# Input projections on raw, unnormalised tokens, with 1/rms put in where results leave PSUM, in a two-layer hybrid trunk on one core

## The chip, the core and the metric

The kernel runs on one core of a Trainium2 chip. A core has five engines with queues of their own: TensorE (PE in the rows; its weight loads are PEld), VectorE (DVE), ScalarE (ACT), GpSimd (POOL) and SyncE (SP), which here only issues DMAs. The metric is the device time of one execution in microseconds (us).

## What is computed

Two layers over one sequence of 2048 tokens, model width 1024, all in float32. Cut to what matters here:

```python
for l in range(DEPTH):                      # DEPTH = 2
    h = rmsnorm(x, norm_g[l])               # x * rsqrt(mean(x*x) + EPS) * g
    z = h @ w_in[l]                         # 1024 -> 2512 columns
    (g_q, g_k, g_v, g_lr, g_gate,           # 256, 256, 512, 16, 512
     c_q, c_kv, k_pe, m_gate) = jnp.split(z, split_idx, axis=-1)   # 256, 128, 64, 512
    log_a = log_sigmoid(g_lr @ w_gla_gate_up[l] + b_gla_gate[l]) / 16
    o_gla = gla_mix(g_q, g_k, g_v, log_a, gla_norm_g[l]) * silu(g_gate)
    # c_q and c_kv go through an RMSNorm of their own, then through w_uq and w_ukv;
    # k_pe gets the rotary turn; causal attention with 4 heads gives o_mla
    o_mla = attention(c_q, c_kv, k_pe) * silu(m_gate)
    x = x + concat([o_gla, o_mla]) @ w_out[l]
```

## The kernel before

Tokens are handled in 16 tiles of 128 (names `t`, `a`, `b`), in 8 pairs `p`; the model width is 8 slices of 128 (index `k`). A float32 product is made of three matmuls on a high and a low part (`mm3`, lines 97 to 99). `block(ps, hT, w, n, ins)` issues the 8 slices of one projection of one tile, 24 matmuls 464 or 512 columns wide, and calls after slice `k` whatever work `ins[k]` lists. So the text of the program sets where each small piece of work stands among the matmuls.

Each layer has four phases. **Pass 1** makes for each pair the blocks `mi a`, `mi b`, `qk a`, `v a`, `qk b`, `v b`. `mi` holds the latents, the rotary key and the 16 low-rank gate columns (columns 448 to 463). `lat_chain(t)` (lines 415 to 433) reads `mi` out of PSUM; its first two operations make `lr`, the gate columns. `gates_a(t)` (line 442) transposes `lr` on TensorE, `gates_b` (449) multiplies it by a small weight `w3r` into `lg`, `gates_c` (458) makes cumulative sums. `gla_b(t)` (476) takes `qk` out of PSUM into `qkp`, which TensorE transposes next. `tail(t)` ends a tile of the linear attention with a normalisation `osn`. **Pass 2** makes the blocks `gt` and `mg` (the two SiLU gates) and the attention queries; a tile's gate output `on` is transposed by TensorE in `out_t`. **Phase b** is the attention, **phase c** the output projection: it writes the new residual stream to the DRAM tensors `xd`, and sums over slices of squares to `sd`.

Before pass 1 uses a tile, the class `Prep` (lines 350 to 396) normalises it. `x` loads the transposed tile, `s` (first layer only) squares it on ScalarE and folds the eight slices into one 128x128 tile `ss` (on VectorE for tile 0, on GpSimd for the others), `n` adds up `ss` over partitions with one matmul by a 128x128 matrix of ones, so that 1/rms comes out for all tokens in every partition (`rb`, 128x128, through a chain of six operations in `rsq`), and `h` (two halves) multiplies the tile by it, splits it into high and low part (`hT`) and writes the normalised tile to the DRAM tensors `hd`, from which pass 2 reads it again. In phase c the same is done ahead for the first two tiles of layer 2.

What sets the order: in pass 1 and pass 2 TensorE follows the program; within the first pair and its loads ScalarE and VectorE do too (`manual_schedule(engines=BOOT)`). Elsewhere a scheduler orders the engines when the kernel is built. SyncE issues DMAs in one queue, in an order that the scheduler sets as well. The input weights are loaded in pieces of two slices, `mi` from two column ranges.

Of the kernel before, what the change touches and what calls it, by code (L numbers as in the profile page):

```python
# [19 lines left out]
P = 128  # L20
# [33 lines left out]
def trunk(ctx: ExitStack, tc: tile.TileContext, xT, positions, norm_g, w_in, w_up, b_up, gla_g,  # L54
# [19 lines left out]
    ones = cp.tile([P, P], F32, name="ones")  # L74
# [4 lines left out]
    sspe = cp.tile([P, NT], F32, name="sspe")  # L79
# [3 lines left out]
    xd = [dp.tile([P, KT, QD], F32, name=f"xd{q}") for q in range(NQD)]  # L83
# [40 lines left out]
    def silu(pool, z, tag, a=None):  # L124
        a = logsig(pool, z, 512, tag, a=a)
# [4 lines left out]
    hd = [dp.tile([P, KT, P], F32, name=f"hd{t}") for t in range(NT)]  # L130
# [217 lines left out]


    class Prep:  # L350
        def __init__(self, l, x_tile, small, psum):
            self.l, self.xt, self.small, self.psum = l, x_tile, small, psum
            self.xs, self.ss, self.rb, self.hT = {}, {}, {}, {}

        def x(self, t):
# [28 lines left out]

        def h(self, t, half):
            if half == 0:
                self.hT[t] = hT_tile("hT")
            hT, xt = self.hT[t], self.xs[t]
            ks = slice(half * 4, half * 4 + 4)
            xv = xt.rearrange("p (k c) -> p k c", k=KT)[:, ks, :]  # L390
            V.tensor_tensor(out=xv, in0=xv, in1=self.rb[t].unsqueeze(1).broadcast_to([P, 4, P]), op=ALU.mult)
            A.activation(out=hT[:, 0, ks, :], in_=xv, func=AF.Copy)
            V.tensor_tensor(out=hT[:, 1, ks, :], in0=xv, in1=hT[:, 0, ks, :].bitcast(F32), op=ALU.subtract)
            if half == 1:
                dma(hd[t].rearrange("p k c -> p (k c)"), xt)
                del self.xs[t], self.rb[t]


    def pass1(l, wp, pp, w1, lat, hT01):
# [8 lines left out]
        prep = Prep(l, lambda name: x_tile(wp, name), w1, lambda: pp.tile([P, P], F32, tag="tp", name="tp"))  # L408
        prep.hT.update(hT01)
        hTs = prep.hT  # L410

        def sq_tile():
            return wp.tile([P, D], F32, tag="stg", name="sq", bufs=3)

        def lat_chain(t, mi):
            lt = lr[:, t % 2]
            V.tensor_copy(lt[:, 0:3:2, 0:16], mi[:, 448:464].unsqueeze(1).broadcast_to([P, 2, 16]))
            V.tensor_tensor(out=lt[:, 1, 0:16], in0=mi[:, 448:464], in1=lt[:, 0, 0:16].bitcast(F32), op=ALU.subtract)
            v2 = w1.tile([P, 2], F32, name="v2")
            jk = w1.tile([P, 256], F32, tag="jk", name="jk", bufs=1)  # L420
            A.activation(out=jk, in_=mi[:, 0:256], func=AF.Square, scale=1.0 / 16.0, accum_out=v2[:, 0:1])
            A.activation(out=jk[:, 0:128], in_=mi[:, 256:384], func=AF.Square, scale=128.0 ** -0.5,
                         accum_out=v2[:, 1:2])
            A.activation(out=jk[:, 128:192], in_=mi[:, 384:448], func=AF.Square, scale=192.0 ** -0.5,
                         accum_out=sspe[:, t:t + 1])
# [6 lines left out]
            V.tensor_tensor(out=kpe[:, t, :], in0=mi[:, 384:448], in1=sm["gkr"], op=ALU.mult)  # L432
# [158 lines left out]
        def sqs(t):  # L591
            return [lambda: prep.s(t, sq_tile(), G)] if l == 0 else []

        def pair(p):
# [5 lines left out]
                  merge(bt[0], tail(a - 1) if p else {}, {0: [go(prep.h, b, 0)], 2: [go(prep.h, b, 1)]} if p else  # L600
                        {2: [go(prep.n, b), go(prep.h, b, 0)], 3: [go(prep.h, b, 1)]} if l == 0 else {}))
# [6 lines left out]
            block(mi, hTs[b], wi["mi"], 464, merge({3 if p else 5: [go(gates_a, a)], 5 if p else 7: [go(gates_b, a)]}, bt[1]))  # L608
# [6 lines left out]
            if not more:  # L615

                for which, blks in (("gt", (2, 3)), ("mg", (4, 5))):
                    pc = wi_pieces(l, which, pool_stage(wp, 2)(512))
# [23 lines left out]
        with tc.manual_schedule(engines=BOOT):  # L642
            if l == 0:
# [7 lines left out]
                for load, _ in pm[1:]:  # L651
                    load()
# [682 lines left out]
```

## Time and profile before

| | us |
|---|---|
| runs of the kernel | 2302.77, 2305.85, 2309.09 (median 2305.85) |
| the profiled execution | 2303.08 |
| its span | 2301.2, mean granted clock 0.995 |
| busy in the span: PE, DVE, ACT, POOL | 2238.2 (97%), 1463.3 (64%), 1328.6 (58%), 452.7 (20%) |
| pass 1 of layer 1 / pass 2 / phase b / phase c | to about 390 / 600 / 985 / 1164 |
| pass 1 of layer 2 / pass 2 / phase b / phase c | to about 1520 / 1700 / 2130 / the end |

The four rows of stages are read from which lines TensorE runs. PE is idle for 63 us in all. The granted clock is a share of TensorE's full speed: 1.00 is 2.4 GHz, 0.50 is 1.2 GHz.

### The profile page before, as it was taken

How to read it: one execution, taken by the hardware profiler on the slowest of the kernel's cores; microseconds unless marked ns; L12 is line 12 of the kernel's file. 1: busy time of each engine (PE TensorE's matmuls, PEld its weight loads, DVE VectorE, ACT ScalarE, POOL GpSimd, SP SyncE). 2: the span in 40 equal slices, each digit the busy share in tenths (PEclk: the TensorE clock that was granted, in tenths of full speed). 3: DMA queues.
4: the chain of work that ended last, by engine and by line, in shares of the span. 5: the costliest groups of instructions: out<-in, count | busy, mean ns of one | idle time of the engine just before them, and what ended most of it. 6: DMA issues, size and time to landing. Idle time of an engine off the chain costs nothing.

```text
span 2301.2 us, 37516 instructions
## 1 busy us (share of the span) xinstructions
PE 2238.2 (97%) x12629; PEld 1931.6 (84%) x12629; DVE 1463.3 (64%) x4456; ACT 1328.6 (58%) x3648; POOL 452.7 (20%) x685
## 2 busy tenths in 40 slices
PE   6999999999999999999999999999999999999999
PEld 4788887888899988888878888878888999988887
DVE  6586676665788887742356566666657888785211
ACT  5465556666777777642245555567667777676100
POOL 1110111333312122132200000033332122123100
PEclk9999999999999999999999999999999999999999
DMA  5121124443311111166432112254432111113542
GB/s 171 46 79 60 47 87 142 129 133 110 108 37 50 31 47 54 51 209 191 146 100 79 61 60 85 75 158 128 134 94 90 31 54 41 33 55 106 176 133 83
DMA packets 186310, 213.09 MB, mean 93 GB/s; under 512 B 18419, under 2 KB 131814, under 8 KB 186118
## 3 DMA queue, kind: packets, MB, share of 16 engines
q1 hardware_dynamic: 185702, 210.58, 29.0%
q8 instruction: 100, 1.64, 0.3%
q14 instruction: 92, 0.75, 0.1%
q0 software_dynamic: 416, 0.12, 0.0%
HBM read 129.91 MB, written 80.74 MB: 92 GB/s over the span
## 4 chain that ended last, share of the span: by engine, by line
PE 87%; ACT 5%; DVE 5%; DMA 1%; issue 1%; POOL 0%; SPq 0%; ACTq 0%; DVEq 0%; POOLq 0%
PE tp L94 8%; PE co L98 5%; PE co L99 5%; PE co L97 5%; PE sp L975 3%; PE sp L978 3%; PE sp L979 3%; PE sp L977 3%; PE sp L976 2%; PE gt L99 2%; PE gt L97 2%; PE gt L98 2%; PE o L1050 2%; PE mg L99 2%; PE mg L97 2%; PE mg L98 2%
## 5 line engine op out<-in xcount | busy, mean ns | idle before, releaser
L98 PE MATMUL co<-y,wo_h 128*128 128x512 f32 x512 | 199.3, 389 | 0.8 <-POOL y L1156 0.8
L97 PE MATMUL co<-y,wo_h 128*128 128x512 f32 x512 | 199.6, 390 | 0.2 <-ACT y L1155 0.2
L99 PE MATMUL co<-y,wo_l 128*128 128x512 f32 x512 | 199.3, 389 | 0.0
L986 DVE TENSOR_SCALAR_CACHE_REDUCE p<-sp 128x512 f32<-128x512 f32 (+5 forms) x304 | 172.9, 572 | 23.0 <-PE sp L979 18.5
L1203 DVE TENSOR_TENSOR xc<-co,xc 128x512 f32<-128x512 f32 x64 | 44.1, 689 | 211.5 <-PE co L99 177.4
L993 ACT ACTIVATE p<-p,nm 128x128 f32<-128x128 f32 (+15 forms) x128 | 154.0, 1204 | 36.4 <-DVE nm L992 30.0
L1029 DVE TENSOR_TENSOR pl<-tp,ph 128x512 fp32r<-128x512 f32 x224 | 151.7, 686 | 35.5 <-ACT ph L1028 34.2
L1050 PE MATMUL o<-pl,v 128*128 128x256 f32 x576 | 170.1, 295 | 2.0 <-DVE pl L1029 1.2
L1048 PE MATMUL o<-ph,v 128*128 128x256 f32 x576 | 167.9, 292 | 4.3 <-ACT ph L1028 2.9
L1028 ACT ACTIVATE ph<-tp 128x512 fp32r<-128x512 f32 x224 | 130.3, 592 | 71.1 <-PE tp L94 63.1
L94 PE MATMUL tp<-cst,p 128*128 128x128 f32 x1088 | 165.7, 274 | 0.3 <-DVE pl L1029 0.2
L1049 PE MATMUL o<-ph,v 128*128 128x256 f32 x576 | 161.1, 280 | 0.0
L975 PE MATMUL sp<-kn,q 128*128 128x512 f32 (+3 forms) x320 | 129.4, 405 | 7.6 <-ACT q L910 5.0
L94 PEld LDWEIGHTS tp<-cst,p 128*128 128x128 f32 x1088 | 124.6, 140 | 8.7 <-DVE pl L1029 1.2
L1048 PEld LDWEIGHTS o<-ph,v 128*128 128x128 f32 x576 | 108.9, 189 | 11.4 <-ACT ph L1028 4.5
L1007 POOL TENSOR_SCALAR gt<-gt,rl 128x128 f32<-128x128 f32 x128 | 78.5, 623 | 195.3 <-DVE rl L1005 108.2
L977 PE MATMUL sp<-kn,q 128*128 128x512 f32 (+3 forms) x320 | 116.4, 370 | 0.0
L976 PE MATMUL sp<-kn,q 128*128 128x512 f32 (+3 forms) x320 | 116.2, 363 | 0.0
L1050 PEld LDWEIGHTS o<-pl,v 128*128 128x128 f32 x576 | 108.6, 189 | 8.2 <-DVE pl L1029 3.6
L978 PE MATMUL sp<-kr,q 128*128 128x512 f32 (+3 forms) x320 | 115.0, 366 | 0.3
L979 PE MATMUL sp<-kr,q 128*128 128x512 f32 (+3 forms) x320 | 114.5, 368 | 0.0
L98 PEld LDWEIGHTS co<-y,wo_h 128*128 128x128 f32 x512 | 96.1, 188 | 21.0 <-POOL y L1156 1.2
(285 smaller groups left out, 6731.1 us busy)
## 6 DMA issues: line engine op xcount, KB each, us to landing
hd<-xt SPq DMA_DIRECT2D x32, 512.0 KB, 2.6
hf<-hd SPq DMA_DIRECT2D x32, 512.0 KB, 3.7
stg<-in_w_in SPq DMA_DIRECT2D x28, 512.0 KB, 4.5
yst<-yd SPq DMA_DIRECT2D x28, 512.0 KB, 5.1
qd<-qs SPq DMA_DIRECT2D x32, 384.0 KB, 3.0
gst<-qd SPq DMA_DIRECT2D x64, 192.0 KB, 2.5
xt<-in_xT SPq DMA_DIRECT2D x16, 512.0 KB, 4.3
od<-osn SPq DMA_DIRECT2D x32, 256.0 KB, 2.1
```

The lines of the kernel that those rows point to most:

```text
L94: T.transpose(o, i, ident[:k, :k])
L97: T.matmul(o, lhsT=lh, rhs=rh, start=start, stop=False)
L98: T.matmul(o, lhsT=lh, rhs=rl, start=False, stop=False)
L99: T.matmul(o, lhsT=ll, rhs=rh, start=False, stop=stop)
L975: T.matmul(o, lhsT=qn[:, 0, ts_], rhs=kn[:, 0, k0:k1], start=True, stop=False)
L976: T.matmul(o, lhsT=qn[:, 0, ts_], rhs=kn[:, 1, k0:k1], start=False, stop=False)
L977: T.matmul(o, lhsT=qn[:, 1, ts_], rhs=kn[:, 0, k0:k1], start=False, stop=False)
L978: T.matmul(o, lhsT=qrr[:, 0, ts_], rhs=kr[:, c0:c1], start=False, stop=False)
L979: T.matmul(o, lhsT=qrr[:, 1, ts_], rhs=kr[:, c0:c1], start=False, stop=True)
L986: V.tensor_scalar(out=pt[:, c0:c0 + w], in0=sp[:, 0:w], scalar1=0.0, scalar2=-3e38, op0=ALU.add, op1=ALU.max, accum_out=mx[:, m:m + 1])
L1048: T.matmul(o[:, s], lhsT=vh, rhs=ph[:, j, s], start=(kb == 0), stop=False)
L1050: T.matmul(o[:, s], lhsT=vh, rhs=pl[:, j, s], start=False, stop=(last and j == 1))
```

## The change

Five things change. (1) `hT` is made from the raw tile: a copy to the high part (ScalarE) and a subtraction (VectorE). 1/rms is kept per token, in three forms in `rt[:, t, 0:3]` (r, r/8, r squared), and applied where projections leave PSUM. (2) The sum of squares: in layer 1 GpSimd squares and folds each tile (`prep_s`), and the reducing matmul has `ss` as stationary side and a 128x2 matrix of ones as moving side, so that 1/rms comes out with one token in each partition. It stands after slice 7 of `mi a` and after slice 6 of `mi b`. In layer 2, one load (`load_s`) and one `norm_q` serve four tiles, after slice 4 of `mi a` in every second pair. (3) The `hd` tensors are gone: pass 2 loads the raw tile. (4) The weights come as five arrays laid out by group, the tokens also as an array `xt` laid out by tile, and `xd` is laid out by tile. (5) The first loads come in another order. In pass 2 the SiLU takes r: its smaller operations are split anew, and one of them goes to GpSimd.

```diff
-        def s(self, t, sq, eng):
-            A.activation(out=sq, in_=self.xs[t], func=AF.Square, scale=1.0 / 32.0)
-            for n in (512, 256):
-                eng.tensor_tensor(out=sq[:, 0:n], in0=sq[:, 0:n], in1=sq[:, n:2 * n], op=ALU.add)
...
-        def n(self, t):
-            ps = self.psum()
-            T.matmul(ps, lhsT=ones, rhs=self.ss.pop(t), start=True, stop=True)
...
-            V.tensor_tensor(out=xv, in0=xv, in1=self.rb[t].unsqueeze(1).broadcast_to([P, 4, P]), op=ALU.mult)
-            A.activation(out=hT[:, 0, ks, :], in_=xv, func=AF.Copy)
-            V.tensor_tensor(out=hT[:, 1, ks, :], in0=xv, in1=hT[:, 0, ks, :].bitcast(F32), op=ALU.subtract)
-            if half == 1:
-                dma(hd[t].rearrange("p k c -> p (k c)"), xt)
+    def split_x(xs, hT, half, lo=None):
...
+        A.activation(out=hT[:, 0, ks, :], in_=xv, func=AF.Copy)
+        (lo or V).tensor_tensor(out=hT[:, 1, ks, :], in0=xv, in1=hT[:, 0, ks, :].bitcast(F32), op=ALU.subtract)
+    def norm(pool, ps, ss, t, n):
+        for i in range(n):
+            T.matmul(ps[:, 2 * i:2 * i + 2], lhsT=ss[:, i * P:(i + 1) * P], rhs=ones, start=True, stop=True)
+        v = pool.tile([P, n], F32, tag=f"xv{n}", name="xv")
+        V.tensor_scalar(out=v, in0=ps[:, 0:2 * n:2], scalar1=1.0 / D, scalar2=EPS, op0=ALU.mult, op1=ALU.add)
+        r = pool.tile([P, n], F32, tag=f"xs{n}", name="xs")
+        rsq(pool, v, n, r, f"xr{n}")
+        V.tensor_copy(rt[:, t:t + n, 0], r)
+        V.tensor_scalar(out=rt[:, t:t + n, 1], in0=r, scalar1=0.125, scalar2=None, op0=ALU.mult)
+        V.tensor_tensor(out=rt[:, t:t + n, 2], in0=r, in1=r, op=ALU.mult)
+        def prep_s(t):
+            sq = wp.tile([P, D], F32, tag="stg", name="sq", bufs=3)
+            G.tensor_tensor(out=sq, in0=xs[t], in1=xs[t], op=ALU.mult)
+            for n in (512, 256):
+                G.tensor_tensor(out=sq[:, 0:n], in0=sq[:, 0:n], in1=sq[:, n:2 * n], op=ALU.add)
+            sss[t] = w1.tile([P, P], F32, tag="ss", name="ss")
+            G.tensor_tensor(out=sss[t], in0=sq[:, 0:P], in1=sq[:, P:2 * P], op=ALU.add)
...
-            V.tensor_copy(lt[:, 0:3:2, 0:16], mi[:, 448:464].unsqueeze(1).broadcast_to([P, 2, 16]))
-            V.tensor_tensor(out=lt[:, 1, 0:16], in0=mi[:, 448:464], in1=lt[:, 0, 0:16].bitcast(F32), op=ALU.subtract)
+            r = rt[:, t, 0:1]
+            V.tensor_scalar(out=lt[:, 0:3:2, 0:16], in0=mi[:, 448:464].unsqueeze(1).broadcast_to([P, 2, 16]),
+                            scalar1=r, scalar2=None, op0=ALU.mult)
...
-            V.scalar_tensor_tensor(out=qkp[:, 0:256], in0=qk[:, 0:256], scalar=0.125, in1=ep,
+            V.scalar_tensor_tensor(out=qkp[:, 0:256], in0=qk[:, 0:256], scalar=rt[:, t, 1:2], in1=ep,
...
-                  merge(bt[0], tail(a - 1) if p else {}, {0: [go(prep.h, b, 0)], 2: [go(prep.h, b, 1)]} if p else
-                        {2: [go(prep.n, b), go(prep.h, b, 0)], 3: [go(prep.h, b, 1)]} if l == 0 else {}))
+                  merge(bt[0], tail(a - 1) if p else {}, {0: [go(prep_h, b, 0)], 2: [go(prep_h, b, 1)]} if p else {},
+                        {7: [go(prep_n, a)]} if l == 0 else {4: [go(norm_q, p // 2)]} if p % 2 == 0 else {}))
...
-            block(mi, hTs[b], wi["mi"], 464, merge({3 if p else 5: [go(gates_a, a)], 5 if p else 7: [go(gates_b, a)]}, bt[1]))
+            if l > 0 and p % 2 == 1 and more:
+                load_s(p // 2 + 1)
+            block(mi, hTs[b], wi["mi"], 464, merge({6: [go(prep_n, b)]} if l == 0 else {}, {3 if p else 5: [go(gates_a, a)], 5 if p else 7: [go(gates_b, a)]}, bt[1]))
...
-                prep.x(0)
+                prep_x(0)
...
-                pm[0][0]()
-                prep.x(1)
-                for load, _ in pm[1:]:
+                for load, _ in pm:
                     load()
+                prep_x(1)
+                for load, _ in pq:
+                    load()
...
-            dma(hf, hd[t].rearrange("p k c -> p (k c)"))
+            dma(hf, x_src(l, t).rearrange("p k c -> p (k c)"))
...
+        a = pool.tile([P, 512], F32, tag=tag, name="ls_a")
+        A.activation(out=a, in_=z, func=AF.Abs, scale=r)
+        A.activation(out=a, in_=a, func=AF.Exp, scale=-1.0)
+        A.activation(out=a, in_=a, func=AF.Ln, bias=1.0)
+        V.tensor_scalar(out=m, in0=z, scalar1=0.0, scalar2=r, op0=ALU.min, op1=ALU.mult)
+        G.tensor_tensor(out=a, in0=m, in1=a, op=ALU.subtract)
         A.activation(out=a, in_=a, func=AF.Exp)
-        V.tensor_tensor(out=a, in0=z, in1=a, op=ALU.mult)
+        V.scalar_tensor_tensor(out=a, in0=z, scalar=r, in1=a, op0=ALU.mult, op1=ALU.mult)
```

The order of instructions on an engine is set when the kernel is built, so it is shown as it comes out; a row gives the line, the operation, what is written and what is read, and the shape.

GpSimd, at the start of the program, behind its small loads; first the kernel before (`sq` and `ss` of tiles 1, 2 and on):

```order
L192 DMA w_204<-in_b_gla_gate 1x16x16
L370 ISA
L370 TENSOR_TENSOR sq<-sq 128x512
L370 TENSOR_TENSOR sq<-sq 128x256
L372 TENSOR_TENSOR ss<-sq 128x128
```

and the changed kernel (an "x2" here is tile 0 and tile 1, one behind the other in each step):

```order
L204 DMA w_196<-in_b_gla_gate 1x16x16
L410 ISA
L410 TENSOR_TENSOR sq<-xt 128x1024 x2
L412 TENSOR_TENSOR sq<-sq 128x512 x2
L412 TENSOR_TENSOR sq<-sq 128x256 x2
L414 TENSOR_TENSOR ss<-sq 128x128 x2
```

Tile 0's sum of squares moved here from VectorE, the squaring moved here from ScalarE, and `ss` of tile 0 stands behind seven operations.

VectorE, first pair, between the end of tile 0's tail and the exit of `qk b`; before (`xv` to `rb` is the 1/rms chain of tile 2, L391 and L393 make its `hT`):

```order
L572 TENSOR_SCALAR osn<-op,r_624 128x128 x4
L380 TENSOR_SCALAR xv<-tp 128x128
L107 TENSOR_TENSOR rq<-ry 128x128
L108 TENSOR_TENSOR rq<-rq,xv 128x128
L109 TENSOR_SCALAR rq<-rq 128x128
L110 TENSOR_TENSOR rb<-ry,rq 128x128
L391 TENSOR_TENSOR xt<-xt,rb 128x512
L393 TENSOR_TENSOR hT<-xt,hT 128x512
L479 SCALAR_TENSOR_TENSOR qkp<-qk,ep 128x256
```

and in the changed kernel:

```order
L589 TENSOR_SCALAR osn<-op,r_606 128x128 x4
L371 TENSOR_TENSOR hT<-xt,hT 128x512
L495 SCALAR_TENSOR_TENSOR qkp<-qk,rt,ep 128x256
```

Six operations between `osn` and `qkp` are gone.

VectorE, second pair, behind the end of `mi a`; before (`lr` are the gate columns; `v`, `rq`, `r` the chain of the tail of the tile before):

```order
L113 TENSOR_SCALAR v_801<-v_801 128x4
L417 CAST lr<-mi 128x2x16
L107 TENSOR_TENSOR rq<-ry 128x4
L418 TENSOR_TENSOR lr<-mi,lr 128x16
L108 TENSOR_TENSOR rq<-rq,v_801 128x4
L109 TENSOR_SCALAR rq<-rq 128x4
L110 TENSOR_TENSOR r_808<-ry,rq 128x4
L572 TENSOR_SCALAR osn<-op,r_808 128x128 x4
```

and in the changed kernel (`xv`, `rq` and `xs` 128x1 are the chain of 1/rms of tile `a`):

```order
L115 TENSOR_SCALAR v_749<-v_749 128x4
L378 TENSOR_SCALAR xv<-tp 128x1
L109 TENSOR_TENSOR rq<-ry 128x4
L110 TENSOR_TENSOR rq<-rq,v_749 128x4
L111 TENSOR_SCALAR rq<-rq 128x4
L109 TENSOR_TENSOR rq<-ry 128x1
L112 TENSOR_TENSOR r_756<-ry,rq 128x4
L110 TENSOR_TENSOR rq<-rq,xv 128x1
L589 TENSOR_SCALAR osn<-op,r_756 128x128 x4
L111 TENSOR_SCALAR rq<-rq 128x1
L112 TENSOR_TENSOR xs<-ry,rq 128x1
L381 COPY rt<-xs 128x1
L382 TENSOR_SCALAR rt<-xs 128x1
L383 TENSOR_TENSOR rt<-xs 128x1
L429 TENSOR_SCALAR lr<-mi,rt 128x2x16
L431 SCALAR_TENSOR_TENSOR lr<-mi,rt,lr 128x16
```

`lr` moved from second and fourth to the last two places, behind the whole chain and behind `osn`. The same order stands in the later pairs.

## Rows read from the trace of the kernel before

**Rows 1.** Page, part 1: busy time, share of the span, instructions.

```profile
PE 2238.2 (97%) x12629; PEld 1931.6 (84%) x12629; DVE 1463.3 (64%) x4456; ACT 1328.6 (58%) x3648; POOL 452.7 (20%) x685
```

**Rows 2.** Waits of PE, 0 to 400 us: sum, times, longest.

```profile
PE tp L94 <- DVE qkp L479: 3.8, 1, 3.8
PE lg L451 <- DVE w3r L220: 2.3, 1, 2.3
```

**Rows 3.** Stretches: length, busy of PE, PEld, DVE, ACT, POOL, clock, DMA share, GB/s.

```profile
80.00:340.00 260.00, 259.03 (x1424) 218.97 (x1425) 178.56 (x539) 147.29 (x461) 31.74 (x36) 1.00 0.19 62
68.00:78.00 10.00, 8.88 (x29) 6.78 (x30) 5.61 (x14) 3.72 (x7) 2.51 (x3) 0.50 0.32 106
1204.00:1214.00 10.00, 8.43 (x37) 6.38 (x37) 7.16 (x21) 4.06 (x9) 0.00 (x0) 0.83 0.33 110
```

**Rows 4.** Timeline of PE: first matmuls of mi b and qk a, pair 0.

```profile
25.53 0.48 PE L97 MATMUL mi<-wmi_h,hT 128*128 128x464 f32 x1 [2.83 <-ACT hT L392]
35.29 0.40 PE L97 MATMUL qk<-wqk_h,hT 128*128 128x512 f32 x1
```

**Rows 5.** Timeline of POOL: its last small load, and foldings of squares.

```profile
9.98 0.48 POOL L192 DMA_DIRECT2D w<-in_b_gla_gate  x1 [0.72 <-DMA qk<-in_k_head_g]
14.34 2.36 POOL L370 TENSOR_TENSOR sq<-sq 128x512 f32<-128x512 f32 x2 [3.88 <-ACT sq L368]
16.78 0.73 POOL L372 TENSOR_TENSOR ss<-sq 128x128 f32<-128x128 f32 x1
59.02 0.45 POOL L372 TENSOR_TENSOR ss<-sq 128x128 f32<-128x128 f32 x1
```

**Rows 6.** POOL's group of 128x512, 0 to 400 us: busy, mean ns.

```profile
L370 POOL TENSOR_TENSOR sq<-sq 128x512 f32<-128x512 f32 x15 | 19.2, 1283 | 281.0 <-ACT sq L368 281.0
```

**Rows 7.** Timeline of DVE and PE at the exit of qk b.

```profile
62.87 1.12 DVE L572 TENSOR_SCALAR osn<-op,r 128x128 f32<-128x128 f32 x4
67.54 0.69 DVE L393 TENSOR_TENSOR hT<-xt,hT 128x512 fp32r<-128x512 f32 x1 [0.69 <-ACT hT L392]
68.15 0.42 DVE L479 SCALAR_TENSOR_TENSOR qkp<-qk,ep 128x256 f32<-128x256 f32 x1
68.62 1.12 PE L94 MATMUL tp<-cst,qkp 128*128 128x128 f32 x4 [3.81 <-DVE qkp L479]
1204.65 1.12 PE L94 MATMUL tp<-cst,qkp 128*128 128x128 f32 x4 [3.81 <-DVE qkp L479]
```

**Rows 8.** Timeline of PE and DVE at the end of mi a, pair 3.

```profile
172.21 0.37 PE L99 MATMUL mi<-wmi_h,hT 128*128 128x464 f32 x1
174.95 0.27 PE L94 MATMUL tp<-cst,lr 128*96 128x128 f32 x1
172.40 0.17 DVE L113 TENSOR_SCALAR v<-v 128x4 f32<-128x4 f32 x1 [0.76 <-ACT jk L564]
173.08 0.17 DVE L107 TENSOR_TENSOR rq<-ry 128x4 f32<-128x4 f32 x1
173.68 0.16 DVE L110 TENSOR_TENSOR r<-ry,rq 128x4 f32<-128x4 f32 x1
174.10 1.12 DVE L572 TENSOR_SCALAR osn<-op,r 128x128 f32<-128x128 f32 x4
```

**Rows 9.** Start of layer 2: SP and PE; a DMA of 256 KB, median landing.

```profile
1166.99 0.32 SPq L60 DMA_DIRECT2D sd<-ac  x1
1167.14 0.37 PE L97 MATMUL mi<-wmi_h,hT 128*128 128x464 f32 x1
on<-od SPq DMA_DIRECT2D x32, 256.0 KB, 2.9
```

**Rows 10.** Timeline of DVE and PE in pass 2, third tile's gate output.

```profile
418.72 0.87 DVE L776 TENSOR_TENSOR on<-on,ls_a 128x512 f32<-128x512 f32 x1
426.11 0.60 PE L94 MATMUL tp<-cst,on 128*128 128x128 f32 x4
```

**Rows 11.** PE's group of the normalising matmul: busy, mean ns.

```profile
L378 PE MATMUL tp<-ss,ones 128*128 128x128 f32 x64 | 13.0, 286 | 8.3 <-DVE ss L372 7.8 <-POOL ss L372 0.5
```

More of the change, by code (lines that the diff above doesn't have):

```diff
@@ L73, in trunk @@
     ind = cst[:, C_IND:C_IND + 2]
-    ones = cp.tile([P, P], F32, name="ones")
+    ones = cp.tile([P, 2], F32, name="ones")
     kpe = cp.tile([P, NT, 64], F32, name="kpe")
@@ L78, in trunk @@
     nsin = cp.tile([P, NT, 32], F32, name="nsin")
-    sspe = cp.tile([P, NT], F32, name="sspe")
+    v3 = cp.tile([P, NT, 3], F32, name="v3")
+    rt = cp.tile([P, NT, 3], F32, name="rt")
     x0 = xT.rearrange("(k p) s -> p k s", p=P)
-    xd = [dp.tile([P, KT, QD], F32, name=f"xd{q}") for q in range(NQD)]
+    xd = [dp.tile([P, 4, KT, P], F32, name=f"xd{q}") for q in range(NQD)]
     sd = [dp.tile([P, QD], F32, name=f"sd{q}") for q in range(NQD)]
@@ L253, in load @@
             r0 = half * 512 + k0 * P
+            if laid:
+                dma(st, src[:, half * 4 + k0:half * 4 + k0 + kk, :])
+                return
             for c, c_src, w in cols:
@@ L407, in pass1, with prep_x @@
         lrTs, las, gts, lns, ops, qks, vps, glas = ({} for _ in range(8))
[L408 to L413, printed above, removed]
+        xs, sss, hTs = {}, {}, dict(hT01)
+        def prep_x(t):
+            xs[t] = x_tile(wp, "xt")
+            for ks in ((slice(0, 512), slice(512, 1024)) if l == 0 and t == 0 else (slice(0, D),)):
+                dma(xs[t][:, ks], x_src(l, t).rearrange("p k c -> p (k c)")[:, ks])
@@ L415, in lat_chain, with prep_n, load_s, norm_q @@
+        def prep_n(t):
+            norm(w1, pp.tile([P, 8], F32, tag="tp", name="tp"), sss.pop(t), t, 1)
+        def load_s(q):
+            sss[q] = w1.tile([P, QD], F32, tag="ss", name="ss", bufs=1)
+            dma(sss[q], sd[q])
+        def norm_q(q):
+            norm(w1, pp.tile([P, 8], F32, tag="tp", name="tp"), sss.pop(q), 4 * q, 4)
         def lat_chain(t, mi):
             lt = lr[:, t % 2]
-            V.tensor_copy(lt[:, 0:3:2, 0:16], mi[:, 448:464].unsqueeze(1).broadcast_to([P, 2, 16]))
@@ L1315, in _consts, with _laid @@
     return c
+def _laid(inputs):
+    a = dict(inputs)
+    a["xT"] = inputs["x"][0].T
+    a["xt"] = np.asarray(inputs["x"][0]).reshape(NT, P, KT, P).transpose(0, 3, 2, 1)
+    w = np.asarray(inputs["w_in"])
+    groups = {"w_mi": np.r_[1552:2000, 1024:1040], "w_qk": np.r_[0:512], "w_v": np.r_[512:1024],
+              "w_gt": np.r_[1040:1552], "w_mg": np.r_[2000:2512]}
+    for name, c in groups.items():
+        a[name] = w[:, :, c].reshape(DEPTH, KT, P, len(c)).transpose(0, 2, 1, 3)
+    return a
 def kernel(**inputs):
```

153 lines of the change are left out of this document (73 added, 80 removed).

## The prediction

> **What bounds the kernel now.** I read the busy times of the page first: TensorE is busy for 97% of the span, the next engine for 64% [rows 1]. Between 80 and 340 us it is idle for 1 us in 260 [rows 3]. So work taken from VectorE, ScalarE or the DMA queues is worth nothing by itself; only TensorE's own work, its clock, and the few places where it waits count. Then I listed its waits up to 400 us, which cover pass 1 of the first layer [rows 2]. Most of them lie in the first 80 us. Two kinds touch the change: the start, where the second block begins at 25.53 after a wait of 2.83 for the normalised tile, and the third at 35.29 after 2.3 for `w3r` [rows 2, 4]; and the exit of `qk b` in the first pair of each layer, 3.81 us for `qkp` [rows 7]. Third, I read the granted clock of short stretches behind such waits: 0.50 for 10 us behind the wait of 3.81 at 68.62, and 0.83 behind the one at 1204.65 [rows 3, 7]. After 2.3 us, on the other hand, the next 512-wide matmul took 0.40 us, as at full speed [rows 2, 4]. So here a wait of 3.8 us also costs clock, one of 2.3 us didn't. All sums are against the profiled execution (span 2301.2, time 2303.08), which lies 2.8 us below the median of 2305.85; the change in time that comes out is then put on the median.
>
> **A. The start.** Before, tile 0 is squared on ScalarE and folded on VectorE. Now `mi a` needs no norm, but the norm matmul stands at its end, ahead of `mi b` on TensorE, and waits for `ss` of tile 0 from GpSimd. GpSimd's small loads end at 10.46 [rows 5]; then come two multiplications of 128x1024, two additions of 512, two of 256, and one of 128, as the order shows. An addition of 512 takes 1.28 us [rows 6], so one of 1024 is an estimate of 2.4 to 2.6; a pair 512 and 256 took 2.36, one of 128 took 0.73 beside a busy VectorE and 0.45 later [rows 5]. Sum: 10.5 + 2 x 2.4 + 2 x 2.36 + 0.6 = 20.6, say 21 with some contention. `mi b` then starts at 21.2 in place of 25.53, and since the wait before it is long it runs partly at half clock again, as now: from 25.53 to 35.29 less the wait of 2.3 are 7.4 us [rows 2, 4]. `w3r` stands behind some 19 small operations on VectorE (about 5 us from 21.2), before `mi b` ends. So `qk a` starts at 28.9 in place of 35.29: **-6**, from -8 (no contention) to 0 (GpSimd 6 us later).
>
> **B. The exit of `qk b`.** Before, between `osn` (62.87, four rows' worth of 1.12) and `qkp` at 68.15 stood the norm chain of the next tile and a multiplication; now only the 0.69 us subtraction for `hT` (its high part is long ready, as the raw tile is). `osn` ends at 63.9, the subtraction at 64.6, `qkp` at 65.05, TensorE starts at 65.1. It was free at 68.62 - 3.81 = 64.81, so the wait falls from 3.81 to about 0.4 [rows 7]. Twice, once per layer: **-6.8**, from -7.6 to -4.
>
> **C. The clock behind it.** A wait of 0.4 us should leave the clock alone. In 68 to 78 the clock was 0.50 with PE busy for 8.88 us, so about 4 us are lost; in 1204 to 1214 it was 0.83, 1.7 us [rows 3]. **-5.7**, down to 0 if the clock falls for another reason.
>
> **D. A new wait for `lr`.** In the first layer's pairs 1 to 7, `lr` of tile `a` now needs 1/rms of that tile, whose matmul stands at the end of `mi a`. TensorE transposes `lr` after slice 3 of `mi b`, 174.95 - 172.21 = 2.74 us after the last matmul of `mi a` began [rows 8]; with the norm matmul of some 0.25 us between, 175.2 in pair 3. VectorE: `v` at 172.40, the chain on four columns from 173.08 in steps of 0.20 [rows 8]; the norm's `xv` at about 172.75 has its ScalarE part done 0.68 later, 173.4, as `v` had. By the new order then come three steps for the four columns, `rq`, `r`, `rq`, so `osn` starts at about 174.3 and ends at 175.3 (1.12 with overlap), and behind it `rq`, `xs`, three copies into `rt`, and two operations for `lr`: seven steps, of which the three independent ones may overlap, 1.0 to 1.4 us. `lr` is there at 176.3 to 176.7, and TensorE waits 1.1 to 1.5, I take 1.3: seven times, **+9**. The bounds are 0 (it starts earlier, as VectorE has less to do ahead of it) and +14 (2 us each). What is queued behind the transpose on TensorE is the rest of `mi b`; nothing there makes up for it later, since the stretch had no idle time [rows 3].
>
> **E. `lr` of tile `b`.** It is needed only in `qk a`, some 5 us later, and is late only in pair 2, where the rotary's 512-wide operations stand ahead on VectorE, and in pair 7 behind a weight split: **+3** (0 to +7).
>
> **F. Pass 2.** The SiLU's subtraction goes to GpSimd, at 1.28 us for 128x512 [rows 6], 62 times; it adds about 0.6 us and two hand-overs to a chain that ends in `on`. `on` was done 6.5 us ahead of its transpose in the third tile [rows 10]. Only the first transposes have no such lead: **+0.7** (0 to +5).
>
> **G. Layer 2.** The norm matmuls of the first four tiles stand after slice 4 of the first `mi a`, at about 1167.1 [rows 9]. They need `sd` to be written (issued 1166.99) and read again; a 256 KB load lands 2.9 us after issue [rows 9]. The store and the load one behind the other would be 5.8 us; but the first quarter of `sd` is the one that is loaded, which was written long before, and only its place in SyncE's queue, behind that store, counts. So the load lands at about 1170, some 2.7 us late, with a little clock: **+4** (0 to +8).
>
> **H. Taken at nothing.** The norm matmul was 286 ns for a record [rows 11], two to a tile, and is replaced by one with two columns, still with a weight load: bounds -0.3 and +0.3 us a tile in one layer, of which I take 0. VectorE loses 64 multiplications and 32 chains on 128x128, ScalarE 16 squares, the DMA queues 32 stores of 512 KB; TensorE's work hides them all, so they give nothing. The weights' longer rows could only help loads that TensorE waits for, which A includes. Phase b comes out in a slightly other order: **0**, -3 to +3.
>
> Here a rule of the Trainium skill speaks against the change. First the rows: one and the same addition of 128 took GpSimd 0.73 us at 16.78, with VectorE busy, and 0.45 at 59.02 [rows 5]. "GPSIMD Engine Reference", section 1, Specifications, says that GpSimd's SBUF interfaces are shared with VectorE, with contention against VectorE instructions that have two SBUF inputs, which the splits of weights in A are; section 4.1 there gives GpSimd about twice VectorE's time for two-input elementwise work. This trace agrees in direction: 0.73 against 0.45, and 1.28 against 0.69 for 128x512 [rows 5, 6, 7]. By that rule all seven operations would stretch, and A would come to nothing.
>
> **Sum:** -6 - 6.8 - 5.7 + 9 + 3 + 0.7 + 4 = -1.8, so 2301.3 against the profiled execution, and **2304** on the median. Adding only half of each unknown's span around it, the case's own range is 2294 to 2313.
>
> **The rivals.**
> R1. *The waits for `lr` don't stand.* If VectorE reaches `v` and `osn` 1.3 us sooner, because two multiplications and a chain ahead of it are gone, D is 0: 2304 - 9 = 2295. For it: VectorE is busy for only 69% of that stretch [rows 3]. Against: `v` waited for ScalarE, not for VectorE's own backlog [rows 8].
> R2. *GpSimd is slowed by VectorE at the start.* By 0.73/0.45 = 1.6 [rows 5] the 10.1 us of A become 16, `ss` comes at 26.6, A is 0: 2310. For it: that row; against: the pair of 512 and 256 took 2.36, against 1.28 for the 512 alone, so it was hardly stretched.
> R3 (slower). *The wait for `lr` costs clock each time.* One mechanism, in pairs 1 to 7 of the first layer: if the wait reaches the 2.83 us which stood ahead of `mi b` (a block of 7.4 us then), each is 1.5 us longer and is followed by some 4 us lost as in C, 7 x 5.5 = +38: 2342. It decides from about 2.3 us up, which cost no clock in [rows 2, 4].
> R4 (slower). *GpSimd's queue makes `on` late in pass 2.* With 62 subtractions between attention's own work there, if a transposed `on` comes 1 us late in about 20 of 32 tiles: 2324. It decides where a gate comes more than 6.5 us later than now [rows 10].
>
> **How the numbers follow.** Forecast 0.52, R1 0.26, R2 0.08, R3 0.06, R4 0.08. A difference of 0.3% (6.9 us) is about what a measurement of this kernel can tell from none: faster is below 2298.9, slower above 2312.8. Of the forecast's 0.52, 0.14 lie below (A at -8, D small), 0.36 between, 0.02 above; of R1 0.23 are faster and 0.03 the same; of R2 0.07 the same and 0.01 slower; R3 and R4 are slower. Together: faster 0.37, same 0.46, slower 0.17. The range takes in the forecast's, R1 with the better bounds of A (2295 - 5 = 2290, rounded to 2289) and R2 with G or F at their worse ends (2310 + 5 = 2315); R3 and R4 with 0.14 are left out, and a little of each tail.
>
> **What would show it.** A: first matmul of `mi b` near 21 and of `qk a` near 29, the norm matmul waiting for GpSimd's `ss`. B, C: no wait above 1 us for `qkp`, clock 1.00 in the 10 us behind it. D: seven waits near 1.3 us of a transpose for `lr`. E: one or two waits in `qk a` of pairs 2 and 7. F: waits for `on` at the start of pass 2 at most 3 us. G: one wait of the norm matmul near 1167. Wrong it would be above all through D (each 0.5 us of it is 3.5 in the sum) and through a fallen clock, which no wait list shows.

## The result, and the profile after

The changed kernel takes 2329.92 us (median of 4 runs, 2326.85 to 2331.26) against 2306.49 for the kernel before (4 runs, 2302.77 to 2309.09). The ratio is 1.0101, with a 95% interval of 1.0083 to 1.0118: slower by 1%, and outside the forecast range of 2289 to 2315. Its profiled execution has a span of 2329.5 us, 28.3 more than before. That is 5 us more than the difference of the medians (23.4), since it is the slowest of the four; the terms below are added up to the 28.3.

The page's busy times:

```profile
PE 2251.2 (97%) x12629; PEld 1934.4 (83%) x12629; DVE 1427.5 (61%) x4421; ACT 1305.0 (56%) x3608; POOL 560.7 (24%) x766
```

PE's waits up to 400 us (sum, times, longest):

```profile
PE tp L96 <- DVE lr L431: 12.2, 8, 1.7
PE tp L96 <- DVE ln L445: 9.5, 7, 3.8
...
PE tp L376 <- POOL ss L414: 3.6, 1, 3.6
...
PE tp L96 <- DVE qkp L495: 0.6, 1, 0.6
```

The long wait for `qkp` of [rows 2] is gone, as forecast. Fifteen waits for `lr` and `ln` have come, 21.7 us together, where the stretch of [rows 3] had 1 us of idle time. Where the time went is read from when blocks begin on PE's timeline:

| first matmul of | before, us | after, us | difference |
|---|---|---|---|
| `qk a`, first pair, layer 1 | 35.29 | 32.35 | -2.9 |
| second pair, layer 1 | 76.96 | 72.53 | -4.4 |
| pass 2, layer 1 | 378.67 | 398.84 | +20.2 |
| pass 1, layer 2 | 1163.98 | 1186.01 | +22.0 |
| `qk a`, first pair, layer 2 | 1174.47 | 1203.54 | +29.1 |
| second pair, layer 2 | 1210.75 | 1235.63 | +24.9 |
| pass 2, layer 2 | 1509.70 | 1536.82 | +27.1 |
| end of the span | 2301.2 | 2329.5 | +28.3 |

So pairs 2 to 8 of the first layer lose 24.6 us, the start of layer 2 loses 7, the start of layer 1 gains 4.4 and the second exit of `qk b` 4.2.

Stretches of the changed kernel (length, busy of PE, PEld, DVE, ACT, POOL, granted clock, DMA share, GB/s):

```profile
412.00:432.00 20.00, 17.31 (x76) 14.29 (x75) 9.10 (x20) 11.87 (x28) 13.28 (x18) 0.91 0.26 89
48.00:60.00 12.00, 9.94 (x39) 7.33 (x38) 3.77 (x8) 5.24 (x12) 4.33 (x4) 0.72 0.00 0
1190.00:1200.00 10.00, 7.68 (x27) 6.91 (x28) 1.84 (x11) 1.56 (x9) 0.00 (x0) 0.66 0.95 337
80.00:340.00 260.00, 239.87 (x1289) 198.59 (x1289) 159.07 (x527) 122.61 (x422) 47.63 (x43) 0.99 0.10 34
140.00:160.00 20.00, 16.18 (x80) 12.95 (x81) 12.19 (x35) 12.18 (x30) 0.00 (x0) 0.91 0.01 2
```

Between 80 and 340 us PE is busy for 239.87 us where it was for 259.03 [rows 3]; the clock there is 0.99, so nearly all of this is waits. The clock falls at 48 to 60, for a short while at 140 to 160, at 1190 to 1200 and early in pass 2.

The timeline of the start: GpSimd, VectorE, and the norm matmul on PE that waits.

```profile
11.07 1.94 POOL L410 TENSOR_TENSOR sq<-xt 128x1024 f32<-128x1024 f32 x1
15.16 1.94 POOL L410 TENSOR_TENSOR sq<-xt 128x1024 f32<-128x1024 f32 x1 [2.16 <-DMA xt<-in_xt]
17.06 5.57 POOL L412 TENSOR_TENSOR sq<-sq 128x512 f32<-128x512 f32 x4
22.60 1.76 POOL L414 TENSOR_TENSOR ss<-sq 128x128 f32<-128x128 f32 x2
...
11.17 8.07 DVE L286 SCALAR_TENSOR_TENSOR wmi_l<-bootmi,g,wmi_h 128x464 fp32r<-128x464 f32 x6
19.17 2.89 DVE L371 TENSOR_TENSOR hT<-xt,hT 128x512 fp32r<-128x512 f32 x2
21.98 3.60 DVE L286 SCALAR_TENSOR_TENSOR wqk_l<-bootqk,g,wqk_h 128x512 fp32r<-128x512 f32 x4
...
23.55 0.38 PE L376 MATMUL tp<-ones,ss 128*128 128x2 f32 x2 [3.55 <-POOL ss L414]
```

`ss` is there at 23.5. In the same stretch two subtractions for `hT` take VectorE 2.89 us, where one took 0.69 [rows 7], and six weight splits take 8.07.

The timeline at the end of `mi a` in the fifth pair, the counterpart of [rows 8] (which are of the fourth), and at the next wait for `ln`:

```profile
222.87 2.11 POOL L412 TENSOR_TENSOR sq<-sq 128x512 f32<-128x512 f32 x2
...
223.35 0.84 DVE L115 TENSOR_SCALAR v<-v 128x4 f32<-128x4 f32 x1 [3.45 <-ACT jk L581]
225.78 1.13 DVE L589 TENSOR_SCALAR osn<-op,r 128x128 f32<-128x128 f32 x4
226.83 0.14 DVE L111 TENSOR_SCALAR rq<-rq 128x1 f32<-128x1 f32 x1
227.68 0.23 DVE L431 SCALAR_TENSOR_TENSOR lr<-mi,rt,lr 128x16 fp32r<-128x16 f32 x1
239.82 0.48 DVE L445 TENSOR_SCALAR ln<-mi,r 128x256 f32<-128x256 f32 x1
...
228.06 0.28 PE L96 MATMUL tp<-cst,lr 128*96 128x128 f32 x1 [1.70 <-DVE lr L431]
240.44 0.52 PE L96 MATMUL tp<-cst,ln 128*128 128x128 f32 x3 [1.08 <-DVE ln L445]
```

`v` took 0.17 in [rows 8]; here it takes 0.84 and ends, at 224.19, about when GpSimd's first addition does (an addition of 512 is 1.28 us of the pair of 2.11 that began at 222.87). `osn` then stands ahead of the rest of the norm's chain, and `lr` is done at 227.9.

The start of layer 2, SP's queue and the norm matmul, and the gate's output in pass 2:

```profile
1189.02 0.33 SPq L60 DMA_DIRECT2D sd<-ac  x1
1189.44 0.38 SPq L60 DMA_DIRECT2D ss<-sd  x1
...
1192.32 1.87 PE L376 MATMUL tp<-ones,ss 128*128 128x2 f32 x8 [2.98 <-DMA ss<-sd]
419.87 0.70 PE L96 MATMUL tp<-cst,on 128*128 128x128 f32 x4 [2.69 <-DVE on L794]
```

### The profile page after: what moved, and what is told of

Same layout as the page of the kernel before. It is cut to its first block, busy times and chain, and to the rows that moved or that the text cites. A ratio compares the mean times of both kernels' runs of the same rounds, so it can differ in the third digit from the quotient of the medians.

```text
span 2329.5 us, 37520 instructions
## 1 busy us (share of the span) xinstructions
PE 2251.2 (97%) x12629; PEld 1934.4 (83%) x12629; DVE 1427.5 (61%) x4421; ACT 1305.0 (56%) x3608; POOL 560.7 (24%) x766
## 4 chain that ended last, share of the span: by engine, by line
PE 84%; DVE 7%; ACT 6%; issue 2%; DMA 2%; POOL 0%; SPq 0%; ACTq 0%; DVEq 0%; POOLq 0%
PE tp L96 8%; PE co L100 5%; PE co L101 5%; PE co L99 5%; PE sp L992 3%; PE sp L995 3%; PE sp L996 2%; PE mg L101 2%; PE mg L99 2%; PE o L1067 2%; PE mg L100 2%; PE sp L994 2%; PE sp L993 2%; PE o L1066 2%; PE vp L99 2%; PE o L1065 2%
## 5 line engine op out<-in xcount | busy, mean ns | idle before, releaser
L909 POOL TENSOR_SCALAR gst<-kpe,rk 128x64 f32<-128x64 f32 x128 | 55.0, 444 | 250.7 <-DVE rk L112 108.1
```

## The experiments

Each was compared with the kernel before on the same chip; the first number is its median, the ratio is to the kernel before.

**Moving the norms.** Two theories of the waits for `lr`: the place of the norm matmul on TensorE, or VectorE's queue.

```diff
-                        {7: [go(prep_n, a)]} if l == 0 else ...
+                        {7 if p == 0 else 5: [go(prep_n, a)]} if l == 0 else ...       # na5; na2: 2
+                        # nb5: {7: a, 5: b}; nab: {2: a, 5: b}, for p > 0
```

na5. 

> One edit: in pairs 1 to 7 of layer 1 the norm matmul of tile a stands after slice 5 of mi a in place of slice 7, 1.27 us earlier. Theory P (the place of the norm matmul sets when lr is ready): the seven waits for lr fall from 1.70 to about 0.4 us, and the time by about 9, to 2321. Theory Q (VectorE's queue sets it, osn stands between the two operations of lr in this build): the waits stay near 1.0 or above, and the time falls by 5 at most, to 2325. The waits for ln stay at 9.5 in sum by both.

Measured: 2325.51 (1.0086, 1.0069 to 1.0102). The waits are 1.12 in six pairs, so theory Q holds: of the 1.27 us by which the matmul came sooner, 0.58 arrived. The timeline shows `osn` between the two operations of `lr`:

```profile
225.12 0.24 DVE L429 TENSOR_SCALAR lr<-mi,rt 128x32 fp32r<-128x32 f32 x1
225.28 1.11 DVE L589 TENSOR_SCALAR osn<-op,r 128x128 f32<-128x128 f32 x4
226.31 0.22 DVE L431 SCALAR_TENSOR_TENSOR lr<-mi,rt,lr 128x16 fp32r<-128x16 f32 x1
...
226.68 0.28 PE L96 MATMUL tp<-cst,lr 128*96 128x128 f32 x1 [1.12 <-DVE lr L431]
```

na2. 

> The same edit with slice 2: the whole chain of 1/rms of tile a lies before the end of mi a, and both operations of lr stand ahead of osn. Both theories: no wait for lr, 12 to 13 us. They part on ln of tile b: if its lateness comes from its own norm after slice 6 of mi b, its 9.5 us stay and the time is about 2317; if it is handed on from the late lr of tile a, they go too and the time is about 2307.

Measured: 2316.18 (1.0042, 1.0030 to 1.0055). PE's waits from 78 to 372 us:

```profile
PE tp L96 <- DVE ln L445: 7.9, 7, 3.5
PE lg L467 <- ACT lrT L462: 1.2, 1, 1.2
PE tp L96 <- DVE lr L431: 1.0, 1, 1.0
```

`lr` of tile a no longer waits; `ln` keeps 7.9 of 9.5 us, so it is late by tile b's own norm.

nb5. 

> The other half alone: the norm matmul of tile b stands after slice 5 of mi a in pairs 1 to 7, that of tile a stays after slice 7. If ln is late by tile b's own norm, the waits for ln (9.5 us, of which one of 3.8 in pair 2 with 2 us of clock behind it) go, those for lr stay at 1.70: about 2319. If ln's lateness is handed on from tile a, about 2330.

Measured: 2319.93 (1.0063, 1.0046 to 1.0080): `ln` falls from 9.5 to 3.2 us, `lr` stays at 1.77. The two halves are separate costs, of about 14 and 10 us.

nab. 

> Both moved: tile a after slice 2 and tile b after slice 5 of mi a. By the theory that the place of the norms costs the 24 us which pairs 1 to 7 lose: no waits for lr and ln left but a small one in pair 2, about 2305, level with the kernel before. By the rival that half of it is the norm matmul itself (a weight load for two columns) or busier queues: not below 2313.

Measured: 2306.33 (1.0005, 0.9995 to 1.0014). From 78 to 372 us `ln` waits once, for 1.4 us, and `lr` never. Pairs 2 to 8 take 304.7 us, where they took 326.3 in the changed kernel and 301.7 before: of the 24.6 us that they lost, 21.6 are back, by the place of the norms alone. The other 3 are not waits (PE waits 3.2 us in these pairs of nab, and waited 3.0 before).

**The norm matmul itself.**

```diff
-            T.matmul(ps[:, 2 * i:2 * i + 2], lhsT=ss[:, i * P:(i + 1) * P], rhs=ones, start=True, stop=True)
+            for _ in range(2):
+                T.matmul(ps[:, 2 * i:2 * i + 2], lhsT=ss[:, i * P:(i + 1) * P], rhs=ones, start=True, stop=True)
```

nab_nn. 

> On the kernel with both norms moved: every norm matmul is issued twice, with the same result, 16 more in each layer. If one costs TensorE 0.2 to 0.3 us, as the blocks of mi suggest (1.15 us longer in the pairs of layer 2 that hold four of them), the time rises by 6 to 9, to about 2314. If they hide beside the other matmuls, as I took it, it stays at 2306.

Measured: 2311.02 (1.0027, 1.0017 to 1.0036), 4.7 above nab (5.1 by the ratios, as nab ran on another chip) for 32 more, 0.15 us each: not hidden, and less than expected. The kernel before paid for 32 such matmuls too [rows 11].

**The start of layer 2**, on nab.

```diff
-                        ... else {4: [go(norm_q, p // 2)]} if p % 2 == 0 else {}))
+                        ... else {7 if p == 0 else 4: [go(norm_q, p // 2)]} if p % 2 == 0 else {}))   # nab_nq7
...
-                load_s(0)
+                sss[0] = ss0                                   # nab_q0: ss0 = kpe[:, 8:16]
+                            ins.setdefault(3, []).append(lambda: dma(ss0, sd[0]))      # in phase c
```

nab_nq7. 

> On the kernel with both norms moved (2306.3): in layer 2 the first norm_q stands after slice 7 of the first mi a in place of slice 4, 1.9 us later. Theory: its wait of 3.0 us for the load of sd falls to about 1.1 and the half clock behind it goes, so the time falls by about 5, to 2301. Rival: 1/rms then comes late for lr, a new wait takes its place, and the time stays at 2306.

Measured: 2302.83 (0.9996, 0.9988 to 1.0005), 3.5 under nab by the medians, 2.1 by the ratios: between the two. Its waits from 1150 to 1250 us show both sides, the load's wait at 1.0 and a longer one for `lrT`:

```profile
PE lg L467 <- ACT lrT L462: 2.9, 2, 1.9
PE tp L376 <- DMA ss<-sd: 1.0, 1, 1.0
```

nab_q0. 

> On the kernel with both norms moved (2306.3): the load of the first quarter of sd for layer 2 is issued during phase c, ahead of the last stores in SyncE's queue, into a part of kpe that is free there; norm_q stays after slice 4. Theory: the 7 us lost in the first mi a and mi b of layer 2 come from that load's place in the queue, so its wait of 3.0 us goes, the half clock behind it too, and no new wait comes: the time falls by 5 to 6, to about 2300.5. Rival: the clock falls there for another reason, or lr is late anyway; then 2303 or more.

Measured: 2299.95 (0.9979, 0.9970 to 0.9988), 6.4 under nab by the medians, 6.0 by the ratios, as expected. From the first `mi a` to `qk a` layer 2 now takes 11.8 us, in nab 17.5, before 10.5.

**Smaller parts.**

```diff
-        G.tensor_tensor(out=a, in0=m, in1=a, op=ALU.subtract)
+        V.tensor_tensor(out=a, in0=m, in1=a, op=ALU.subtract)     # nab_silv
```

nab_silv. 

> On the kernel with both norms moved: the SiLU's subtraction is on VectorE in place of GpSimd. If GpSimd's slower subtraction costs the waits at the start of pass 2 (2.7 us for on, twice, once per layer, of which the kernel before had 2.1 and 2.6), about 1 us at most comes back: 2305. If it were the queue of GpSimd over the whole of pass 2, 3 us or more would.

Measured: 2306.34 (1.0005, 0.9996 to 1.0015): no change in the time. The waits for `on` are 3.5 and 2.8, in nab 2.7 and 2.7, so with the subtraction on VectorE the first of them is longer, not shorter. Neither reading shows; for the time the engine of the subtraction doesn't matter.

lay (the kernel before, with the weight arrays laid out by group). 

> The kernel before with one part of the change alone: the input weights laid out by group, loaded in the old order. As TensorE waits only about 3 us for weights in all, I expect 2303 to 2306, no difference that can be told; by the rival that longer rows speed up the first loads, mi a and v a come earlier and the time falls by 4 or more, to 2302 or less.

Measured: 2306.89 (1.0008, 0.9998 to 1.0017): no difference, as expected. Longer rows buy nothing here.

**The start of layer 1.**

```diff
-                prep_s(1)                                     # nab_gs0: behind slice 7 of mi a
+                boot.update({(0, 4): [pq[0][1]], (0, 7): [go(prep_s, 1)], (0, 6): [pq[1][1]], (1, 2): [pq[2][1]],
...
-            block(mi, hTs[b], wi["mi"], 464, merge({6: [go(prep_n, b)]} if l == 0 else {}, ...
+            block(mi, hTs[b], wi["mi"], 464, merge({3: [go(prep_n, b)]} ...         # nab_q0_b3, p == 0
```

nab_gs0. 

> On the kernel with both norms moved: tile 1's squares are asked for after slice 7 of mi a, so that GpSimd does tile 0's five operations first. The sum of squares of tile 0 comes near 17 us in place of 23.5. Theory S (the start is carried through): mi b and qk a come up to 3 us earlier and so does the second pair; about 2303. Theory W (v a waits for its weights, which are split at a time of their own): the second pair starts where it did, within 1 us, and the time stays near 2306.

Measured: 2305.55 (1.0004, 0.9995 to 1.0013). `ss` of tile 0 comes at 17.6 and yet the second pair starts at 73.65 (73.18 in nab). That seemed to bear theory W out. But VectorE's row gives another reason, six splits in 10.18 us (8.07 in the changed kernel), and in sqav, below, the second pair does move:

```profile
11.84 10.18 DVE L286 SCALAR_TENSOR_TENSOR wmi_l<-bootmi,g,wmi_h 128x464 fp32r<-128x464 f32 x6
```

nab_q0_b3. 

> The same, and in the first pair the norm matmul of tile b stands after slice 3 of mi b in place of slice 6, so that on VectorE its chain comes ahead of the last split of the qk weights. Theory W says that what follows the first pair hangs on the order on VectorE and ScalarE: lr of tile b and the splits of v's weights come 1 to 2 us sooner, the wait of v a shrinks: 1 to 4 us under the kernel without it. Rival: the weights of v land or are staged late themselves: no difference.

Measured: 2298.81 (0.9977, 0.9967 to 0.9986), 1.1 under nab_q0, well inside both intervals: undecided.

**GpSimd's squares.** The order of VectorE at the places in question stays; GpSimd's work is taken away from there.

```diff
-            sq = wp.tile([P, D], F32, tag="stg", name="sq", bufs=3)
+            sq = w1.tile([P, D], F32, tag="sq", name="sq", bufs=1)           # sqw1
...
-            G.tensor_tensor(out=sq, in0=xs[t], in1=xs[t], op=ALU.mult)       # sqav: the adds on V too
+            A.activation(out=sq, in_=xs[t], func=AF.Square)
```

sqw1. 

> The changed kernel with one edit: in pass 1 the squares have a buffer of their own, so GpSimd needn't wait for the linear attention to release one and works in the qk b and v b blocks, not at the end of mi a. The order on VectorE in pass 1 is the same. Theory G (GpSimd's operations hold up VectorE's small ones): v of 0.84 us in the chain before lr comes back to 0.17, the waits for lr fall from 1.70 to about 1.0, 5 us in sum or a little more with the waits for ln; about 2324. Theory P (only the order counts): the waits stay at 1.70 and the time at 2330.

Measured: 2345.05 (1.0171, 1.0157 to 1.0185), a miss: the waits for `lr` fall to 0.91 as theory G has it, but those for `ln` rise from 9.5 to 15.7 and the clock from 80 to 340 us falls to 0.97. GpSimd's work went to another place that matters, and it is tied to TensorE there: in the fifth pair its last addition, `ss`, waits 10.07 us for a norm matmul. There, too, VectorE is held up: `rq`, 128x4, takes 1.47 us beside a GpSimd multiplication that ends with it.

sqav. 

> The changed kernel with the squares on ScalarE and their folding on VectorE, nothing on GpSimd. The order at the end of mi a is the same as in the changed kernel. Theory G: the same gain in the waits for lr, to about 1.0, and the start, too, has its sum of squares sooner (before 20 us); about 2322. Theory P: lr stays at 1.70, and VectorE's 2.3 us a tile more make no difference or a loss: 2330 or more.

Measured: 2319.37 (1.0065, 1.0051 to 1.0079), 10.6 under the changed kernel by the medians, 8.3 by the ratios. The waits for `lr` are 0.74 to 0.75 in the pairs that had 1.70 (but for the last pair, 1.63), the waits for `ln` are as they were, and the start gains most: the second pair begins at 65.70, 6.8 sooner than in the changed kernel. VectorE's start on the timeline, against that of the changed kernel above:

```profile
12.43 2.75 DVE L286 SCALAR_TENSOR_TENSOR wmi_l<-bootmi,g,wmi_h 128x464 fp32r<-128x464 f32 x4
15.10 1.28 DVE L371 TENSOR_TENSOR hT<-xt,hT 128x512 fp32r<-128x512 f32 x2
...
17.89 2.73 DVE L286 SCALAR_TENSOR_TENSOR wqk_l<-bootqk,g,wqk_h 128x512 fp32r<-128x512 f32 x4
```

A weight split takes 0.69 us in place of 1.35, the two subtractions 1.28 in place of 2.89. Not all of the 6.8 us is GpSimd's: from 48 to 60 us this execution had the clock at 1.00, the changed kernel's at 0.72, which is 3.4 us, and that can differ between executions that wait alike (C, below).

**All together.** q0_sqw1 is nab_q0_b3 with sqw1's edit; best is nab_q0_b3 with sqav's, best_k6 is nab_q0 with sqav's.

q0_sqw1. 

> All repairs together: both norms early, the load of sd early, the first pair's tile b after slice 3, squares with a buffer of their own. The waits for lr and ln are nearly gone without the last one (1.4 us for ln in pair 2), so by either theory the time is 2297 to 2300; by theory G up to 2 us under nab_q0_b3.

Measured: 2310.33 (1.0021, 1.0012 to 1.0031), worse than nab_q0_b3: sqw1's fault again, `lg` waits 5.6 and `lr` 3.1 us in the first pair.

best. 

> nab_q0_b3 (2298.8) with the squares on ScalarE and their folding on VectorE, as in sqav. If GpSimd's squares cost the start some 7 us there too (second pair at 72.5, in sqav at 65.7), about 2292, a clear gain on the kernel before. If the start was slow for what stands in VectorE's queue, or the folding gets in the way of qkp and hT, 2297 or more.

best_k6. 

> nab_q0 (2300.0) with the squares on ScalarE and their folding on VectorE; the first pair's tile b keeps its norm after slice 6, as in sqav, which lost no time to lg there. About 2292 too; against best it tells whether the earlier norm in the first pair, which left lg a wait of 3.9 us, is worth anything: 2 us either way.

Measured: best 2297.67 (0.9965, 0.9952 to 0.9977), best_k6 2296.85 (0.9962, 0.9949 to 0.9976). Both beat the kernel before. In best's profiled execution (span 2291.3) the second pair starts at 66.0, as in sqav, so the gain at the start is there; but this is the fastest of its five runs, which spread to 2300.8, and the median has kept less of it than expected. In best_k6, whose first pair has its norms where sqav has them, the second pair starts at 69.4, with the clock at 0.72 from 48 to 60 us, where best and sqav had 1.00. At the same clock the changed kernel starts it at 72.53, so about half of sqav's 6.8 us was clock. Which norm is better in the first pair stays undecided.

## Why the prediction was wrong

Two steps failed, A at the start and E in pairs 2 to 8. C's loss of clock moved to another place, and D, G and H were set too small.

| term | forecast | measured |
|---|---|---|
| A, B and C in layer 1 | -13.4 | -4.4 |
| D, `lr` of tile a | +9 | 11.8 of waits, of 24.6 in pairs 2 to 8 |
| E, tile b | +3 | 9.9 of waits and about 2 of clock, of the same 24.6 |
| F, pass 2 | +0.7 | +1.9 up to layer 2 |
| G, start of layer 2 | +4 | +7.0 |
| B and C in layer 2 | -5.1 | -4.2 |
| H, the rest | 0 | +3.4 |

(Half of B, -3.4, belongs to each layer; C was 4 in the first and 1.7 in the second. H is the difference of 24.9 and 28.3 in the table of blocks.)

**A failed.** Its step was "10.5 + 2 x 2.4 + 2 x 2.36 + 0.6 = 20.6, say 21 with some contention". `ss` came at 23.5: the multiplications were cheaper (1.94 each, where 2.4 was taken), the additions dearer (5.57 for 4.72), and GpSimd waited 2.16 for tile 1, which the sum left out. Above all, only one side of the contention was counted. [rows 5] and rival R2 speak of GpSimd slowed by VectorE. It is VectorE that lost more: its splits took twice as long, and all that stands behind them was late. sqav, with the squares taken off GpSimd, starts `qk a` at 27.55, 7.7 us before the old kernel, where A had 6: the gain was there to be had. Its second pair begins 11.3 us before the old kernel's; in best_k6, where the clock fell at 48 to 60 us, 7.5. Doing tile 0 first on GpSimd (nab_gs0) didn't help, since VectorE was held up all the same.

The trace shows the form of it. In nab an operation of VectorE on a single column, with two inputs in memory, begins just behind a multiplication of GpSimd and ends with it:

```profile
210.05 1.89 POOL L410 TENSOR_TENSOR sq<-xt 128x1024 f32<-128x1024 f32 x1 [9.95 <-PE op L573]
...
210.10 1.86 DVE L112 TENSOR_TENSOR xs<-ry,rq 128x1 f32<-128x1 f32 x1
```

The Trainium skill, "SBUF — State Buffer", section "SBUF: two separate sides", says that VectorE and GpSimd share a pair of ports, that whichever starts first holds it for its whole instruction, and that the other is fully blocked, if VectorE's has two inputs in SBUF or runs in a two-port mode. This trace agrees for this row: 1.86 us for what takes 0.16 alone.

**B was right** (waits of 0.60 and 0.5, forecast 0.4). **C was right about its place and wrong about the sum:** behind `qkp` the clock stayed, but it fell behind the wait of `v a` for its weights, 1.77 us at 50.73, in 48 to 60 us (0.72). Before, a wait of 1.70 at that place left it alone. So the rule read from [rows 3, 4], that 2.3 us cost no clock and 3.8 do, does not hold: the length of a wait alone does not decide. The same wait can go either way; first the changed kernel, then two rows of nab_silv, whose wait is as long:

```profile
50.73 0.49 PE L99 MATMUL vp<-wv_h,hT 128*128 128x512 f32 x1 [1.77 <-ACT wv_h L285]
...
51.38 0.50 PE L99 MATMUL vp<-wv_h,hT 128*128 128x512 f32 x1 [1.77 <-ACT wv_h L285]
48.00:60.00 12.00, 9.69 (x53) 7.25 (x52) 5.33 (x10) 5.87 (x14) 6.22 (x5) 1.00 0.00 0
```

The 4 us of C were such a single reading, too: lay, with the same wait of 3.81 for `qkp` at 68.62, had the clock at 0.83 from 68 to 78 us, where the kernel before had 0.50 [rows 3].

**D was right in mechanism and too small:** 1.70 in six pairs and 1.63 in the last, where 1.3 was taken. Without GpSimd beside it the wait is 0.74 (sqav), below the 1.1 to 1.5 that the steps gave; the other 0.96 is VectorE held up (`v` alone takes 0.84 there and 0.17 in sqav). That it was no matter of the matmul's place alone, but of `osn` in VectorE's queue, as the order showed, is what na5 shows.

**E failed, and it is the other large miss:** "needed only in `qk a`, some 5 us later". That is true of `lr` of tile b. But 1/rms of tile b also goes into `v` and `r2` and so into `ln`, which TensorE transposes early in `v a`, and the chain to it is longer by the norm. `ln` was not costed at all: 1.07 us in five pairs, 3.82 in the third behind the rotary, with the clock at 0.91 behind it. nb5 and na2 show that this is tile b's norm and not handed on from D.

**G was right in place**, with a wait of 2.98 where 2.7 was taken; mis-sized is "a little clock", which was 0.66 over 10 us. nab_q0 takes it away. **F** came as a wait of 2.69 (2.1 before) with the clock at 0.91 behind it; nab has the same wait and no loss up to layer 2, so the cause of that 1.9 is not settled. **H** was right for the weights (lay) and wrong to take the rest at nothing. Of the 3.4 us, 2.2 arise in pass 1 of layer 2, and they are TensorE's own time: PE waits no longer there than before (1.2 us, before 1.7) at a clock of 1.00. `mi a` of the third pair, which holds four norm matmuls, runs from 1278.01 to 1286.61, 8.60 us, where it took 7.44 before. That lies within the bounds that H gave the norm matmul, of which it took 0. The other 1.2 were not followed up.

R3 did not come: seven waits of 1.63 to 1.70 cost clock in none of the pairs (0.99 from 80 to 340 us, with the one of 3.82 in it). R4 did not come. R1's condition, no wait for `lr`, holds in nab with the norms moved ahead, but not its time: 2306, where R1 had 2295, as A, C, G and H fell short there, too.

## What to carry to other kernels

When an operand's scale is moved to the far side of a matmul, list every reader of the scaled result and when TensorE needs each of them: the scale must be ready before the first, and here it had been ready for free. Place such a short reduction a block ahead, not at the end of the block that needs it. And when work is given to GpSimd because it is idle, count the VectorE operations that will stand still beside it.

## What the runs showed of the hardware

VectorE's small two-input operations beside GpSimd's took 1.86 us (128x1) and 1.47 (128x4) in place of 0.16, ending with GpSimd's instruction; even an operation with one input tile, 128x4, took 0.84 in place of 0.17. Matmuls in float32 that move only two columns behind a weight load of 128x128 cost TensorE about 0.15 us each in the sum (nab_nn). And a wait of 1.77 us at 50.73 was followed by half clock (0.72 from 48 to 60 us), while the same wait in nab_silv was not (1.00), nor were waits of 1.70 in six later pairs: from one execution the cost of a short wait in clock can't be told.
